# A decoder block on one core: 36 of the 44 up tiles of its two FFNs by seven half-size products instead of eight

## The chip, the cores and the metric

The kernel runs on one core of a Trainium2 chip. Its time is the device time of one execution in microseconds, the median of its runs. The profile is of one execution, with its own time. Engines are named as the profile names them: PE (matrix products) and PEld (its weight loads), DVE, ACT, POOL, and SP, which only issues DMAs here. A name with a q behind it is the engine's sequencer.

## The reference, cut to what matters

The block has a half-step SwiGLU FFN, a token-mixing layer (attention, a causal convolution, gates) and a second half-step SwiGLU FFN, over 512 tokens of width 1024. The FFN's hidden width is 2816. Each of the three is followed by a layer norm, and each is modulated by shift, scale and gate rows that come from a conditioning vector c by one product with `w_ada` (1024 x 9216).

```python
def swiglu(u, w_gu, w_down):
    a, g = jnp.split(u @ w_gu, 2, axis=-1)
    return (jax.nn.silu(a) * g) @ w_down

def reference(x, c, w_ada, b_ada, ffn1_w_gu, ...):
    mod = (jax.nn.silu(c) @ w_ada[l] + b_ada[l]).reshape(bsz, N_SUBLAYERS * N_MOD, 1, D_MODEL)
    sh1, sc1, g1, sh2, sc2, g2, sh3, sc3, g3 = [mod[:, i] for i in range(N_SUBLAYERS * N_MOD)]
    ...
    u = x * (1.0 + sc3) + sh3
    x = layer_norm(DEEPNORM_ALPHA * x + g3 * (MACARON_WEIGHT * swiglu(u, ffn2_w_gu[l], ffn2_w_down[l])), ...)
    return x
```

## The kernel before

**Precision.** Every float32 operand of a product is split into a high part, which PE's fast float format holds exactly, and the rest. A product of two matrices is then three matmuls per block of 128 channels: high by high, high by low, low by high (`dense`, L140 to L146). The tokens `u` are kept transposed, as `uh` and `ul`, eight blocks of 128 channels by 512 tokens.

**An FFN's up stage.** The hidden width is 22 tiles of 128. For a tile, two weight blocks of 128x1024 (512 KB each, one for a, one for g) are loaded by SP into the ring `raw` (3 buffers); ACT writes the high part `whi` (L113), POOL the low part `wlo` (L114), each in a ring of 5. PE makes 48 matmuls of 512 columns into two PSUM banks. Then ACT applies Silu (L396) and DVE multiplies by g from PSUM (L397); the result is the tile `sF`, kept in SBUF. The first FFN's first four tiles run together with the computation of u, while the weights arrive (`first_group`, L462 to L466). The second FFN's first two tiles are one group of products on 256 columns each, since u comes in four quarters of 128 tokens.

**Background work.** The rows of shift, scale and gate are made beside the up tiles by a queue of small tasks: `bg(n)` runs the next n of them in program order, `prefetch(n)` issues loads. A task is either one 128x1024 multiply-add on DVE (L222) or two 128x512 multiplications with a sum (L189), each on one 512 KB load of SP, held in a ring of three buffers (`ADA`). In the first FFN 32 such tasks make g1, g2, sh2 and sc2; in the second, 8 make g3 (ring of two). `load_x` brings in the four x tiles, which ACT scales (L491), and `finish_x(2)` multiplies and adds the layer norm's rows to them on POOL beside the second FFN's up tiles.

**An FFN's down stage** (`down`). For each of 22 hidden tiles, POOL multiplies the weight block by the gate row (L137), ACT writes its high part, DVE its low part, `part` splits `sF` into `sh` (ACT, L419) and `sl` (DVE, L420), and PE makes 24 matmuls (L355) into eight PSUM banks that stay open to the end. The rings of `sh` and `sl` hold five tiles each, and the casts of the first five `sF` run early in the up stage, as soon as those tiles exist.

**What sets the order.** The kernel is written in program order; a scheduler then orders each engine's instructions ahead of the run by its own estimates, subject to data, buffer and stated dependencies. Each engine runs its list in that order, so an instruction that waits holds up all behind it on its engine.

## Time and profile before

| | |
|---|---|
| median of 3 runs | 1339.79 us (1338.65 to 1344.78) |
| the profiled execution | 1338.98 us, span 1337.3 us, mean granted PE clock 0.992 |
| first FFN: start and u; up tiles 4 to 21; down | 0 to 66.7 us; to 264.5 us; to 374 us |
| mixing layer, with its output product | to 971.9 us |
| second FFN: up tiles; down and the last layer norm | to 1208.5 us; to 1337.3 us |
| moved by DMA | 197.88 MB |

The span is the time from the first instruction to the last; the execution's own time is 1.7 us longer. A timeline's row reads: start, duration, engine, line, operation, output <- inputs, shape; a bracket holds the idle time ahead of it and what released it. Matmuls overlap: what counts is the time from start to start. A row of a line's own view gives least, median and largest duration in ns. A row of windows gives for each stretch the busy time of PE, PEld, DVE, ACT and POOL with the number of instructions, then the granted clock, the DMA engines' busy share and GB/s.

### The profile page before, as it was taken

The numbers are of one execution on the slowest core, as the hardware profiler recorded it, in microseconds if no ns is written. First come the engines' busy times: TensorE is split into PE (matmuls) and PEld (weight loads), VectorE is DVE, ScalarE is ACT, GpSimd is POOL, SyncE is SP. The second block draws the span as 40 slices with busy tenths as digits, with TensorE's granted clock in tenths as the row PEclk, the third lists the DMA queues.
The fourth block names the chain that finished last, engine by engine and source line by source line (L and its number), as shares of the span: only waits on it lengthen the run. The fifth ranks groups of instructions, "written<-read, shape, count | busy, mean of one in ns | idle before, by whom it ended". The sixth has DMA issues, their size and how long they took to land.

```text
span 1337.3 us, 16794 instructions
## 1 busy us (share of the span) xinstructions
PE 1292.0 (97%) x6444; PEld 1069.7 (80%) x6444; DVE 737.6 (55%) x1017; ACT 523.0 (39%) x793; POOL 570.9 (43%) x392
## 2 busy tenths in 40 slices
PE   5899999999999999999999998998999999999997
PEld 4688888888898878778778876887898888888885
DVE  7886830354463959598788977025672000025545
ACT  2233322222266554655565547432452222222220
POOL 3465444744312565543442111142254566564434
PEclk9999999999999999999999998998999999999999
DMA  9668843223337574755567997972183233333321
GB/s 356 215 216 310 295 155 95 95 95 104 88 92 189 112 158 94 169 121 123 109 142 151 257 248 196 208 168 79 52 294 95 95 110 95 113 105 92 101 64 63
DMA packets 57856, 197.88 MB, mean 148 GB/s; under 512 B 6688, under 2 KB 6832, under 8 KB 57776
## 3 DMA queue, kind: packets, MB, share of 16 engines
q1 hardware_dynamic: 47952, 161.15, 36.3%
q0 software_dynamic: 9824, 35.66, 15.8%
q8 instruction: 50, 0.82, 0.2%
q14 instruction: 30, 0.25, 0.1%
HBM read 194.70 MB, written 2.10 MB: 147 GB/s over the span
## 4 chain that ended last, share of the span: by engine, by line
PE 82%; DVE 12%; DMA 3%; ACT 1%; POOL 1%; issue 1%; SPq 0%; DVEq 0%; POOLq 0%; ACTq 0%
PE y L355 19%; DVE cacc L525 4%; DVE ada L189 3%; DMA ada<-in_ada_t 1%; PE z L628 1%; PE q L144 1%; PE glub L144 1%; PE glua L144 1%; PE pw L650 1%; PE ycv L146 1%; PE gb L146 1%; PE gb L144 1%; PE ycv L144 1%; PE gb L145 1%; PE ycv L145 1%; PE q L145 1%
## 5 line engine op out<-in xcount | busy, mean ns | idle before, releaser
L114 POOL TENSOR_TENSOR wlo<-raw,whi 128x1024 fp32r<-128x1024 f32 x88 | 224.5, 2556 | 250.9 <-ACT whi L113 237.3
L113 ACT CAST whi<-raw 128x1024 fp32r<-128x1024 f32 x144 | 149.6, 1046 | 274.8 <-issue 50.6
L137 POOL TENSOR_TENSOR raw<-raw,mod_g 128x1024 f32<-128x1024 f32 x52 | 131.4, 2530 | 140.2 <-DMA raw<-in_dn 79.3
L525 DVE SCALAR_TENSOR_TENSOR cacc<-h,cv_w,cacc 128x512 f32<-128x512 f32 x232 | 173.8, 807 | 0.0
L114 DVE TENSOR_TENSOR wlo<-raw,whi 128x1024 fp32r<-128x1024 f32 x56 | 106.5, 1902 | 26.7 <-ACT whi L113 26.7
L130 ACT CAST whi<-raw 128x1024 fp32r<-128x1024 f32 x68 | 71.4, 1049 | 126.7 <-PE ga L145 19.7
L355 PE MATMUL y<-whi,sh 128*128 128x512 f32 x352 | 113.7, 390 | 0.0
L355 PE MATMUL y<-whi,sl 128*128 128x512 f32 x352 | 113.6, 389 | 0.0
L355 PE MATMUL y<-wlo,sh 128*128 128x512 f32 x352 | 113.6, 389 | 0.0
L189 DVE SCALAR_TENSOR_TENSOR ada<-ada,crow 128x512 f32<-128x512 f32 x96 | 91.7, 993 | 25.8 <-DMA ada<-in_ada_t 20.5
L640 POOL TENSOR_TENSOR be<-be,nb 128x127 f32<-128x127 f32 (+1 forms) x64 | 55.1, 861 | 102.0 <-DVE nb L635 100.5
L420 DVE TENSOR_TENSOR sl<-sF,sh 128x512 fp32r<-128x512 f32 x44 | 45.3, 1031 | 85.1 <-ACT sh L419 85.1
L419 ACT CAST sh<-sF 128x512 fp32r<-128x512 f32 x44 | 27.1, 623 | 144.4 <-PE y L355 132.0
L355 PEld LDWEIGHTS y<-whi,sl 128*128 128x128 f32 x352 | 66.1, 188 | 13.8
L355 PEld LDWEIGHTS y<-whi,sh 128*128 128x128 f32 x352 | 66.1, 188 | 13.6
L355 PEld LDWEIGHTS y<-wlo,sh 128*128 128x128 f32 x352 | 66.1, 188 | 13.6
L132 POOL DMA_DIRECT2D wlo<-in_w_in x44 | 38.4, 874 | 82.1 <-ACT wlo L131 78.3
L131 ACT ACTIVATE wlo<-whi 128x1024 fp32r<-128x1024 f32 x68 | 72.1, 1060 | 0.9
L635 DVE TENSOR_TENSOR_SCAN nb<-nb,future 128x127 f32<-128x127 f32 (+1 forms) x64 | 60.2, 941 | 2.0 <-ACT nb L633 1.8
L638 POOL TENSOR_SCALAR_AFFINE_SELECT be<-be 128x128 f32<-128x128 f32 x64 | 44.2, 691 | 22.9 <-ACT be L634 22.3
L222 DVE SCALAR_TENSOR_TENSOR acc<-ada,silu_c,acc 128x1024 f32<-128x1024 f32 x21 | 42.6, 2029 | 12.9 <-DMA ada<-in_ada_w 12.7
L654 DVE TENSOR_TENSOR wTl<-pw,wTh 128x128 fp32r<-128x128 f32 (+1 forms) x64 | 30.5, 477 | 32.5 <-ACT wTh L653 32.4
(496 smaller groups left out, 3366.8 us busy)
## 6 DMA issues: line engine op xcount, KB each, us to landing
raw<-in_gu SPq DMA_DIRECT2D x80, 512.0 KB, 3.6
raw<-in_w_in SPq DMA_DIRECT2D x48, 512.0 KB, 3.7
raw<-in_dn SPq DMA_DIRECT2D x44, 512.0 KB, 3.5
wlo<-in_w_in POOLq DMA_DIRECT2D x44, 512.0 KB, 7.1
ada<-in_ada_t SPq DMA_DIRECT2D x32, 512.0 KB, 5.3
ada<-in_ada_w SPq DMA_DIRECT2D x24, 512.0 KB, 4.9
ada<-in_ada SPq DMA_DIRECT2D x32, 256.0 KB, 6.0
raw<-in_gu_first SPq DMA_DIRECT2D x8, 512.0 KB, 6.5
```

Source lines behind the costliest of these rows:

```text
L113: nc.scalar.copy(hi, raw)
L114: lo_eng.tensor_sub(lo, raw, hi.bitcast(F32))
L130: nc.scalar.copy(hi, raw)
L131: nc.scalar.mul(lo, hi.bitcast(F32), -1.0)
L137: nc.gpsimd.tensor_mul(raw, raw, G)
L144: nc.tensor.matmul(ps[:, c0:c1], wh[:, ks], mov(uh, k)[:, c0:c1], start=(k == 0), stop=False)
L189: nc.vector.scalar_tensor_tensor(raw[:, qs], raw[:, qs], 1.0, crow[:, qs], ALU.mult, ALU.mult, accum_out=parts[:, q : q + 1])
L355: nc.tensor.matmul(acc[t][h][:, c0 - h * 512 : c1 - h * 512], st[:, tsl], wt[:, c0:c1], start=(k == 0 and i == 0 and c0 % 512 == 0), stop= ...
L420: nc.vector.tensor_sub(sl, sF[f], sh.bitcast(F32))
L525: ins = nc.vector.scalar_tensor_tensor(o, hv, cv_w[:, j, i : i + 1], o, ALU.mult, ALU.add)
L635: nc.vector.tensor_tensor_scan(nb[:, 1:n][:, ::-1], nb[:, 1:n][:, ::-1], future[:, S - n + 1 : S][:, ::-1], 1.0, ALU.mult, ALU.max)
L640: nc.gpsimd.tensor_mul(be[:, 0 : n - 1], be[:, 0 : n - 1], nb[:, 1:n])
```

## The change

The weights and tokens of an up tile's product are cut into 2x2 blocks: the weights into a and g (rows) by the first and last 512 input channels (columns), the tokens into those channels by the first and last 256 tokens. Eight block products make a tile; Strassen's algorithm, in Winograd's form, needs seven, on sums and differences of blocks. The two FFNs' tiles from the pair on (6 to 21 in the first, 2 to 21 in the second, 36 in all) go this way; the others are made as before.

- **Products** (`product`, L513). Seven groups of 12 matmuls with 256 columns: 84 instead of 48 with 512. Three PSUM banks per tile: q collects P1, P6, P7, P4 in turn without being cleared, v has P2, z collects P5 and P3. ACT copies q's partial sum out three times (`copied`, 128x256); DVE adds the parts (L540, L553, L562), ACT applies Silu to the whole tile, and DVE multiplies by g in two halves (L564 from PSUM, L565).
- **Weights** (`prep`, L486). Each tile needs seven weight halves of 128x512: A11, A12, A22 as loaded, and S1 to S4. ACT writes all seven high parts. The low parts of S1 and S3 are made on DVE, of S2 and S4 on POOL (`LO_POOL`, L503). For A11, A12 and A22, ACT writes the negated high part and POOL issues a DMA that adds the weights from memory to it (256 KB each, L501). POOL makes S1 and S2 in place (L505, L506), DVE S3 and S4 (L508, L509). A half is prepared nine products ahead; ten half slots in the rings; a fourth `raw` buffer; a tile's two loads are issued when S4 of the tile two before it is done.
- **Tokens** (`strassen_tokens`). The four sums of token blocks are made once for each FFN: 20 instructions of 128x512 on DVE, 8 on POOL, 8 casts on ACT (`replace`, which writes the last sum over u's second half, is among them). In the first FFN they stand ahead of the pair's products in the program and run beside these; in the second they come behind the pair.
- **Room.** In the first FFN the sums T1 and T2 lie where the x tiles lie later, so `load_x` moves into the down stage (k = 4, 6, 8, 10 in program order). `sh` and `sl` lie in a pool that opens when the up stage's own pool is closed. `finish_x(2)` moves to DVE in the second FFN's down stage, one task per k. The ring for g3's loads has one buffer instead of two.

In the lists below, as the scheduler left them, a row has the line, the operation, and output <- inputs with the tile's number behind each name. Where the program's line is the same in both versions, it stands a few lines later in the new one (L114 is L116, L189 is L192, L222 is L225).

POOL at the start of the first FFN's Strassen tiles, new: the last two low parts of the pair (`wlo_608`, `wlo_614`), token sums (`tsum`), S1 of the first two tiles (L505), and as the last row the first adding DMA.

```order
L430 TENSOR_TENSOR tsum_525<-ul_80 128x512
L432 TENSOR_TENSOR tsum_527<-uh_79 128x512
L116 TENSOR_TENSOR wlo_608<-raw_605,whi_607 128x1024
L434 TENSOR_TENSOR tsum_526<-ul_80 128x512
L437 TENSOR_TENSOR tsum_527<-tsum_527,tsum_526 128x512
L116 TENSOR_TENSOR wlo_614<-raw_611,whi_613 128x1024
L505 TENSOR_TENSOR raw4_743<-raw4_743 128x512
L430 TENSOR_TENSOR tsum_531<-ul_80 128x512
L432 TENSOR_TENSOR tsum_533<-uh_79 128x512
L505 TENSOR_TENSOR raw_741<-raw_741 128x512
L434 TENSOR_TENSOR tsum_532<-ul_80 128x512
L501 DMA wlo_735<-in_gu1 128x512
```

The same place before: from the second low part of tile 4 on, only low parts stand there.

```order
L114 TENSOR_TENSOR wlo_549<-raw_546,whi_548 128x1024
L114 TENSOR_TENSOR wlo_615<-raw_612,whi_614 128x1024
L114 TENSOR_TENSOR wlo_621<-raw_618,whi_620 128x1024
L114 TENSOR_TENSOR wlo_684<-raw_681,whi_683 128x1024
L114 TENSOR_TENSOR wlo_690<-raw_687,whi_689 128x1024
```

`wlo_735` is the low part of A11, the first product's weights; the DMA that completes it now stands behind seven token sums, two block sums and the pair's low parts.

DVE over one of the first FFN's Strassen tiles, new: sums of parts (L540, L553, L562), S3 and S4 (L509), low parts (L503), the products with g (L564, L565), and four background tasks (L225, L192).

```order
L540 TENSOR_TENSOR sF9_1118<-c1_1133,v_1116 128x256
L553 TENSOR_TENSOR u3_1109<-u3_1109,z_990 128x256
L509 TENSOR_TENSOR raw_740<-raw_741,raw_740 128x512
L225 SCALAR_TENSOR_TENSOR acc_1508<-ada_1768,silu_c_66,acc_1508 128x1024
L503 TENSOR_TENSOR wlo_735<-raw_740,whi_730 128x512
L225 SCALAR_TENSOR_TENSOR acc_1508<-ada_1895,silu_c_66,acc_1508 128x1024
L192 SCALAR_TENSOR_TENSOR ada_2021,parts_2160<-ada_2021,crow_84 128x512
L562 TENSOR_TENSOR sF8_991<-u2_1057,z_990 128x256
L192 SCALAR_TENSOR_TENSOR ada_2021,parts_2160<-ada_2021,crow_84 128x512
L564 TENSOR_TENSOR sF8_991<-sF8_991,q_988 128x256
L565 TENSOR_TENSOR sF8_991<-sF8_991,u3_1109 128x256
L503 TENSOR_TENSOR wlo_737<-raw_741,whi_732 128x512
```

Before, between the products with g of tiles 8 and 9 (a row with x2 stands for two alike):

```order
L397 TENSOR_TENSOR sF8_882<-sF8_882,h8g_833 128x512
L189 SCALAR_TENSOR_TENSOR ada_1475,parts_1469<-ada_1475,crow_84 128x512 x2
L189 SCALAR_TENSOR_TENSOR ada_1477,parts_1469<-ada_1477,crow_84 128x512 x2
L189 SCALAR_TENSOR_TENSOR ada_1548,parts_1469<-ada_1548,crow_84 128x512 x2
L189 SCALAR_TENSOR_TENSOR ada_1620,parts_1469<-ada_1620,crow_84 128x512
L397 TENSOR_TENSOR sF9_950<-sF9_950,h9g_901 128x512
```

In both, some four background tasks stand to a tile at this place, more than the one or two that the program's own order has; in the new list low parts and block sums that PE's next products need stand between and behind them.

ACT at the end of the first FFN's up stage, new: L563 is the last tile's Silu, L699 scales an x tile, L627 is the cast to `sh`.

```order
L699 ACTIVATE x3_3264<-x3_3264 128x1024
L115 CAST whi_3001<-raw_2998 128x1024
L563 ACTIVATE sF21_2685<-sF21_2685 128x512
L699 ACTIVATE x0_3033<-x0_3033 128x1024
L627 CAST sh_2857<-sF0_534 128x512
L627 CAST sh_2892<-sF1_537 128x512
```

The same place before; the casts of the first five `sF` stand some sixty rows earlier:

```order
L396 ACTIVATE sF20_1757<-h20a_1707 128x512
L113 CAST whi_1928<-raw_1925 128x1024
L113 CAST whi_1963<-raw_1960 128x1024
L396 ACTIVATE sF21_1831<-h21a_1781 128x512
L113 CAST whi_2002<-raw_1999 128x1024
L419 CAST sh_2041<-sF5_674 128x512
```

The first operand of the down stage, `sh_2857`, is now cast behind the last Silu and behind the scaling of x0.

The diff, cut to its core:

```diff
--- before.py
+++ after.py
...
+LOAD_X = (4, 6, 8, 10)
+LO_POOL = ("S2", "S4")
...
-    def finish_x(which):
+    def finish_x(which, pool=None):
...
-            row[v] = raw_tile(a[f"ln{which}_{v}"].broadcast_to([P, D]))
+            src = a[f"ln{which}_{v}"].broadcast_to([P, D])
+            if pool is None:
+                row[v] = raw_tile(src)
+            else:
+                row[v] = pool.tile([P, D], F32, tag="r", name="lnrow", bufs=2)
+                load(row[v], src)
...
+            eng = nc.gpsimd if pool is None else nc.vector
+            op = eng.tensor_mul if v == "g" else eng.tensor_add
...
-    def down(nk, part, w_src, G, tok_done):
+    def down(nk, part, w_src, G, tok_done, every=False):
...
-            if k % 2:
+            if k % 2 or every:
                 bg(1)
+            if nk == NF and not every and k in LOAD_X:
+                load_x(LOAD_X.index(k))
...
+    def make_temps(fp):
+        state["temps"] = [fp.tile([P, S], F32, tag="sF", name="tsum", bufs=NF) for _ in range(12)]
+    def strassen_tokens(up, u, homes):
+        uh, ul = u
...
+        v, g = nc.vector, nc.gpsimd
+        later = []
+        for c in range(2):
+            cs = slice(2 * c, 2 * c + 2)
+            f1, f2, f4, g1, g2, f3 = [t.rearrange("p (k s) -> p k s", k=2) for t in state["temps"][6 * c : 6 * c + 6]]
...
+            v.tensor_sub(f1, h["12"], h["11"])
+            g.tensor_sub(g1, l["12"], l["11"])
+            v.tensor_add(f1, f1, g1)
+            g.tensor_sub(f3, h["22"], h["12"])
+            v.tensor_sub(f2, h["22"], f1)
+            g.tensor_sub(g2, l["22"], l["12"])
+            v.tensor_add(f2, f2, l["22"])
+            v.tensor_sub(f4, h["21"], f2)
+            g.tensor_add(f3, f3, g2)
+            v.tensor_add(f4, f4, l["21"])
+            for x, f in (("2", f2), ("1", f1), ("4", f4)):
+                nc.scalar.copy(th[x], f)
+                v.tensor_sub(tl[x], f, th[x].bitcast(F32))
+            later.append((cs, f3, h["12"]))
+        def replace():
+            for cs, f3, h12 in later:
+                nc.scalar.copy(H["12"][:, cs], f3)
+                v.tensor_sub(L["12"][:, cs], f3, h12)
...
+        return replace, {"P1": part("11"), "P2": part("21"), "P3": part("22"), "P4": both("4"), "P5": both("1"),
+                "P6": both("2"), "P7": part("12")}
+    def strassen(up, fp, which, wgu, js, T, sF, between):
+        his = [wts.tile([P, 1024], F32R, align_bytes=256, tag="whi", name="whi", bufs=5) for _ in range(5)]
+        los = [wts.tile([P, 1024], F32R, align_bytes=256, tag="wlo", name="wlo", bufs=5) for _ in range(5)]
+        raws = [wts.tile([P, 1024], F32, tag="raw", name="raw", bufs=3) for _ in range(3)]
+        raws.append(up.tile([P, 1024], F32, name="raw4"))
...
+        order = []
+        for i in range(len(js) + 1):
+            order += [(x, k) for x, k in (("A11", i), ("A12", i), ("S1", i - 1), ("S2", i), ("A22", i - 1),
+                                          ("S4", i - 1), ("S3", i)) if 0 <= k < len(js)]
...
+            ra, rg = raws[2 * i % 4], raws[(2 * i + 1) % 4]
+            load(ra, a[wgu][js[i], 0])
+            load(rg, a[wgu][js[i], 1])
+            quarters[i] = {"A11": ra[:, :512], "A12": ra[:, 512:], "A21": rg[:, :512], "A22": rg[:, 512:]}
+        def prep(n):
...
+            x, i = order[n]
+            if n == 0:
+                fetch(0)
+                fetch(1)
+            q = quarters[i]
+            hi, lo = W[x, i] = slot(n)
+            r = q[{"S1": "A21", "S2": "A11", "S3": "A11", "S4": "A12"}.get(x, x)]
+            nc.scalar.copy(hi, r)
+            if x[0] == "A":
...
+                nc.scalar.mul(lo, hi.bitcast(F32), -1.0)
+                nc.gpsimd.dma_start(out=lo, in_=src, accum_op=ALU.add)
+            else:
+                (nc.gpsimd if x in LO_POOL else nc.vector).tensor_sub(lo, r, hi.bitcast(F32))
+            if x == "A12":
+                nc.gpsimd.tensor_add(q["A21"], q["A21"], q["A22"])
+                nc.gpsimd.tensor_sub(q["A11"], q["A21"], q["A11"])
+            elif x == "S2":
+                nc.vector.tensor_sub(q["A12"], q["A12"], q["A11"])
+                nc.vector.tensor_sub(q["A11"], q["A22"], q["A11"])
+            elif x == "S4":
+                fetch(i + 2)
+        def product(i, p, ps, x, first):
+            prep(st["n"] + 9)
+            st["n"] += 1
+            wh, wl = W.pop((x, i))
+            more = {} if first else {"skip_group_check": True}
+            for k in range(4):
+                ks = slice(k * P, (k + 1) * P)
+                th, tl = T[p](k)
+                nc.tensor.matmul(ps[:, :256], wh[:, ks], th, start=(first and k == 0), stop=False, **more)
+                nc.tensor.matmul(ps[:, :256], wh[:, ks], tl, start=False, stop=False, **more)
+                nc.tensor.matmul(ps[:, :256], wl[:, ks], th, start=False, stop=(k == 3), **more)
...
+        def P1(i):
+            st[i] = {x: bank(x) for x in "qvz"}
+            st[i]["s"] = fp.tile([P, S], F32, tag="sF", name=f"sF{js[i]}", bufs=NF)
+            product(i, "P1", st[i]["q"], "A11", True)
+            st[i]["c1"] = copied(st[i]["q"], "c1")
+        def P2(i):
+            d = st[i]
+            product(i, "P2", d["v"], "A12", True)
+            nc.vector.tensor_add(d["s"][:, :256], d["c1"], d["v"][:, :256])
+        def P6(i):
+            product(i, "P6", st[i]["q"], "S2", False)
+            st[i]["u2"] = copied(st[i]["q"], "u2")
...
+        def P5(i):
+            d = st[i]
+            product(i, "P5", d["z"], "S1", True)
+            nc.vector.tensor_add(d["u3"], d["u3"], d["z"][:, :256])
+        def P3(i):
+            d = st.pop(i)
+            product(i, "P3", d["z"], "S4", False)
+            s = d["s"]
+            nc.vector.tensor_add(s[:, 256:], d["u2"], d["z"][:, :256])
+            nc.scalar.activation(s, s, AF.Silu)
+            nc.vector.tensor_mul(s[:, :256], s[:, :256], d["q"][:, :256])
+            nc.vector.tensor_mul(s[:, 256:], s[:, 256:], d["u3"])
+            sF[js[i]] = s
+        st["n"] = 0
+        for n in range(9):
+            prep(n)
+        for i in range(len(js) + 1):
+            between(i, True)
+            for f, k in ((P1, i), (P2, i), (P5, i - 1), (P6, i), (P4, i - 1), (P3, i - 1), (P7, i)):
+                if 0 <= k < len(js):
+                    f(k)
+            between(i, False)
     def ffn(which, u, wgu, wdn, gate, first_done, tok_done):
...
-            while j < NF:
-                first = which == 2 and j < 2
-                n = 1 + j % 2 if which == 1 else 1
-                prefetch(n)
...
+            if which == 2:
+                make_temps(fp)
+                j = 0
+            up_cm, up = open_pool(f"up{which}")
+            def home(x, p):
+                if which == 1 and x in "12":
+                    return core.tile([P, 4, 256], F32R, tag=f"x{2 * '12'.index(x) + 'hl'.index(p)}", name=f"T{x}{p}")
+                return up.tile([P, 4, 256], F32R, name=f"T{x}{p}")
...
+            if which == 1:
+                replace, T = strassen_tokens(up, u, home)
+            prefetch(1)
+            pss = dense_group(names, srcs, u, which == 2)
...
+            if which == 2:
+                replace, T = strassen_tokens(up, u, home)
+            replace()
+            j += 2
+            def between(i, before):
+                n = 1 + (which == 1 and i % 3 != 0)
+                (prefetch if before else bg)(n if which == 1 or len(background) > 2 * NT else 0)
+            strassen(up, fp, which, wgu, list(range(j, NF)), T, sF, between)
+            close_pool(up_cm)
+            dn_cm, dp = open_pool(f"dn{which}")
+            state["dp"] = dp
 
...
-                sh = fp.tile([P, S], F32R, align_bytes=256, tag="sh", name="sh", bufs=RES + 1)
-                sl = fp.tile([P, S], F32R, align_bytes=256, tag="sl", name="sl", bufs=RES + 1)
+                sh = dp.tile([P, S], F32R, align_bytes=256, tag="sh", name="sh", bufs=RES + 1)
+                sl = dp.tile([P, S], F32R, align_bytes=256, tag="sl", name="sl", bufs=RES + 1)
...
-            down(NF, part, lambda f: a[wdn][f], mods[gate], tok_done)
+            down(NF, part, lambda f: a[wdn][f], mods[gate], tok_done, which == 2)
+            close_pool(dn_cm)
...
-        ada_row(lnp3, ada_ring(lnp3, 2), lnp3, "g3", 2, 0.5)
-        background.extend(finish_x(2))
+        ada_row(lnp3, ada_ring(lnp3, 1), lnp3, "g3", 2, 0.5)
+        background.extend(finish_x(2, lnp3))
...
-                last["rows"] = ln_rows(lnp3, 3)
+                last["rows"] = ln_rows(state["dp"], 3)
...
```

More of the change, by code (lines that the diff above doesn't have):

```diff
@@ L400, in ffn @@
             j = first_done(gated, fp)
-            while j < NF:
-                first = which == 2 and j < 2
-                n = 1 + j % 2 if which == 1 else 1
-                prefetch(n)
-                pairs = [j, j + 1] if first else [j]
-                names = [f"h{i}{x}" for i in pairs for x in "ag"]
-                srcs = [a[wgu][i, x] for i in pairs for x in range(2)]
-                pss = dense_group(names, srcs, u, first)
-                for q, i in enumerate(pairs):
-                    gated(i, pss[2 * q], pss[2 * q + 1])
-                j += len(pairs)
-                bg(n)
-                if which == 1 and j > NF - 2 * NT and j % 2:
-                    load_x(j // 2 - (NF // 2 - NT))
+            if which == 2:
+                make_temps(fp)
+                j = 0
@@ new lines, in ffn @@
+            up_cm, up = open_pool(f"up{which}")
[3 more added lines that the diff above has]
+                return up.tile([P, 4, 256], F32R, name=f"T{x}{p}")
+            pairs = [j, j + 1]
+            names = [f"h{i}{x}" for i in pairs for x in "ag"]
+            srcs = [a[wgu][i, x] for i in pairs for x in range(2)]
+            if which == 1:
+                replace, T = strassen_tokens(up, u, home)
```

42 lines of the change are left out of this document (40 added, 2 removed).

## The prediction

> **What bounds the kernel now.** The page's busy times and its chain come first.
>
> ```profile
> PE 1292.0 (97%) x6444; PEld 1069.7 (80%) x6444; DVE 737.6 (55%) x1017; ACT 523.0 (39%) x793; POOL 570.9 (43%) x392
> PE 82%; DVE 12%; DMA 3%; ACT 1%; POOL 1%; issue 1%; SPq 0%; DVEq 0%; POOLq 0%; ACTq 0%
> ```
>
> PE is busy for 97% of the span and holds 82% of the chain. The windows by stage say whether that holds where the change is: the two up stages, then two short stretches with dense DMA. Columns: length, PE, PEld, DVE, ACT, POOL, granted clock, DMA share, GB/s.
>
> ```profile
> 66.68:264.47 197.79, 197.79 (x873) 163.72 (x872) 103.78 (x123) 58.94 (x71) 106.98 (x41) 1.00 0.57 197
> 971.90:1208.40 236.50, 236.13 (x1111) 198.31 (x1110) 52.05 (x45) 68.90 (x87) 134.63 (x54) 1.00 0.39 127
> 100.00:134.00 34.00, 34.00 (x151) 28.15 (x150) 23.84 (x20) 10.85 (x13) 17.80 (x7) 1.00 0.86 311
> 735.00:770.00 35.00, 35.00 (x156) 29.00 (x155) 31.82 (x56) 20.93 (x23) 5.31 (x6) 1.00 0.98 252
> ```
>
> In both up stages PE never pauses and the clock is full, so fewer PE cycles are worth their full length there, as long as the others keep up. But the first FFN's early tiles already have DVE at 23.84 of 34 us and DMA at 0.86: that is where the slack is thin.
>
> **What the change removes.** Starts of matmuls, from PE's timeline: the first of tile 4 and of tile 5, 48 matmuls of 512 columns apart; and the first and last of 48 matmuls of 256 columns in the second FFN's pair.
>
> ```profile
> 66.68 0.39 PE L144 MATMUL h4a<-uh,whi 128*128 128x512 f32 x1
> 77.56 0.39 PE L144 MATMUL h5a<-uh,whi 128*128 128x512 f32 x1
> 88.44 0.39 PE L144 MATMUL h6a<-uh,whi 128*128 128x512 f32 x1
> ...
> 972.10 0.28 PE L145 MATMUL h1a<-ul,whi 128*128 128x256 f32 x1
> 977.74 0.28 PE L144 MATMUL h0a<-uh,whi 128*128 128x256 f32 x1
> 989.87 0.40 PE L144 MATMUL h2a<-uh,whi 128*128 128x512 f32 x1
> ```
>
> A tile takes 77.56 - 66.68 = 10.88 us, 0.2267 us a matmul. With 256 columns, (977.74 - 972.10) / 47 = 0.120 us, in the very pattern of weights (high, high, low) that the new products have. So a Strassen tile is 84 x 0.120 = 10.08 us, and 36 tiles save 36 x 0.80 = **28.8 us**: an eighth fewer products, of which the halved width gives part back (0.120 against 0.113).
>
> **What a tile now asks of the other engines.** Rows for each kind of instruction, and two from the DMA views (queue: packets, MB, share of 16 engines; the first over 66 to 170 us, the second over the run).
>
> ```profile
> L189 DVE SCALAR_TENSOR_TENSOR ada<-ada,crow x96: 635/682/2912, 6.8 to 833.3; 128x512 f32<-128x512 f32 x96
> L222 DVE SCALAR_TENSOR_TENSOR acc<-ada,silu_c,acc x21: 1273/1289/3417, 71.3 to 999.6; 128x1024 f32<-128x1024 f32 x21
> L420 DVE TENSOR_TENSOR sl<-sF,sh x44: 681/693/2901, 68.8 to 1301.4; 128x512 fp32r<-128x512 f32 x44
> L654 DVE TENSOR_TENSOR wTl<-pw,wTh x64: 258/474/693, 435.4 to 725.0; 128x128 fp32r<-128x128 f32 x16, 128x256 fp32r<-128x256 f32 x16, 128x384 fp32r<-128x384 f32 x16, 128x512 fp32r<-128x512 f32 x16
> L337 POOL TENSOR_TENSOR o<-o,lnb 128x512 f32<-128x512 f32 x2 | 2.6, 1281 | 0.2
> L132 POOL DMA_DIRECT2D wlo<-in_w_in x44: 856/875/892, 408.2 to 871.0; - x44
> DMA to landing us min/median/max: 5.4/6.9/9.7
> L419 ACT CAST sh<-sF x44: 619/622/642, 68.2 to 1300.7; 128x512 fp32r<-128x512 f32 x44
> q1 hardware_dynamic: 7826, 28.48, 77.8%
> q0 software_dynamic: 9824, 35.66, 15.8%
> ```
>
> ACT: seven casts, three negations and a Silu of 512 at 0.62 and three copies of 256 at about 0.4 (between 0.26 and 0.69 of L654's widths): 8.0 us of 10.08. POOL: four sums at 1.28 and three DMA issues at 0.88: 7.8 us. DVE: four of 512 at 0.69 and five of 256 at 0.4: 4.8 us. DMA: queue q1 was busy 77.8% of 104 us for 54.3 loads of 512 KB, 1.49 us each; q0, which adds to what lies there, 15.8% of 1337.3 us for 68 of 512 KB, 1.55 us per 256 KB. So a tile is 2 x 1.49 + 3 x 1.55 = 7.6 us. Each fits, though none by much. About 26 tiles carry nothing else; I cost them at **1 us** together (0 to 8: were one engine to need 10.4 us, 26 x 0.3). This hides under PE; ACT is the nearest to showing.
>
> The down stage of the second FFN gets the work of `finish_x(2)` on DVE, eight tasks of 1.3 us: L420's and the low part's 1.9 us leave over 2 us of a k's 5.4. No cost.
>
> **The first FFN's early tiles.** Here four background tasks stand in each tile, for some seven tiles. Each is one 1.29 or two 0.68: with the ends overlapping as the rows above allow, some 1.25 us. DVE is then at 4.8 + 4 x 1.25 = 9.8 us of 10.08. Two rows show what a collision with POOL costs (POOL's four L114, DVE's three L222, in the same stretch):
>
> ```profile
> 85.57 12.21 POOL L114 TENSOR_TENSOR wlo<-raw,whi 128x1024 fp32r<-128x1024 f32 x4 [3.36 <-ACT whi L113]
> 85.18 7.97 DVE L222 SCALAR_TENSOR_TENSOR acc<-ada,silu_c,acc 128x1024 f32<-128x1024 f32 x3
> ...
> L114 POOL TENSOR_TENSOR wlo<-raw,whi x88: 2388/2402/3398, 11.2 to 1188.3; 128x1024 fp32r<-128x1024 f32 x88
> L397 DVE TENSOR_TENSOR sF<-sF,h4g x2: 673/681/689, 83.2 to 1022.8; 128x512 f32<-128x512 f32 x2
> ```
>
> Undisturbed, DVE's three are 3.9 us and POOL's four 9.6; together they take 12.2, so each DVE instruction put (12.21 - 9.61) / 3 = 0.87 us into POOL's row, and waited up to (7.97 - 3.87) / 3 = 1.4 us itself, over half of a POOL instruction. L397, with one operand from PSUM, never stretched. POOL's four sums in a tile would hold DVE for about 4 x 1.28 x 0.57 = 2.9 us, at most 5.1, if each meets one; half of them do, by DVE's share: 1.5. So DVE needs 11.3 us, 1.2 over PE's. DMA needs 7.6 + 4 x 1.49 = 13.6 us, or, at the 413 GB/s of its best slices (below), 3.9 MB in 9.5 us: between 0 and 3.5 over. DVE's own list is what turns lateness into a PE wait: L553 must have read bank z before P3 may go on in it, and only two products, 2.9 us, stand between. The lead of nine halves doesn't help there; nor is it there yet after the start below. Whatever of the two is later holds a tile by 1.2 to 3.5 us, seven times, less 2.9: 5.5 to 21. I take **12 us**, about the middle; low end 0, where DMA keeps its best rate and the collisions stay few.
>
> ```profile
> DMA packets 7833, 28.57 MB, mean 275 GB/s; under 512 B 874, under 2 KB 874, under 8 KB 7826
> GB/s 181 285 202 0 126 413 361 296 14 202 153 303 225 343 321 356 366 328 258 326 359 399 296 72 399 214 405 413 386 175 350 243 321 293 307 262 142 224 326 343
> ```
>
> The mean over those 104 us (275) and the slices of 2.6 us (413 at best, over 350 for three in a row at most) say how far 3.9 MB in 10 us, 390 GB/s, lies from what was held for long.
>
> **Start of the first FFN's tiles.** The third matmul of P1 needs the DMA behind the token sums of POOL's list. Today POOL does the pair's second low part at:
>
> ```profile
> 68.37 2.41 POOL L114 TENSOR_TENSOR wlo<-raw,whi 128x1024 fp32r<-128x1024 f32 x1 [2.03 <-ACT whi L113]
> ```
>
> From there three low parts (7.2) and nine sums (9 x 1.28 = 11.5) lead to 87.1, and landing takes 5.4 at the least (512 KB; half of it may be quicker, say 4): 91 to 92.5, where PE is ready at 88.44 plus 0.24. That is 2.4 to 3.8 us with no collision. DVE's 18 token sums run meanwhile; if each of POOL's nine meets one and loses 0.87 / 1.29 x 0.69 = 0.47 us, it is 4.2 more; up to 0.69 each and on the low parts too, 8.3. The second DMA, 0.9 + 1.3 us behind the first, costs another 0.8 over P1's 1.44. And a PE idle this long loses its clock:
>
> ```profile
> 806.99 1.12 PE L797 MATMUL ptb<-ident,cn 128*128 128x128 f32 x4 [7.26 <-DVE cn L786]
> ...
> 809.61 0.63 PE L145 MATMUL ysb<-pl,whi 128*128 128x512 f32 x1
> 810.04 0.63 PE L146 MATMUL ysb<-ph,wlo 128*128 128x512 f32 x1
> ```
>
> After 7.26 us of idleness the 512-column matmuls start 0.43 us apart, not 0.23, for the rest of some 6 us: about 2.8 us lost. The Trainium skill (TensorE: Matmul & The Clock Gate, HAM oscillation) says that idle gaps over about 3.4 us bring the slow clock; this row agrees. I take 3.2 + 4.2 + 0.8 + 1.8 = **10 us** (2.5 to 16).
>
> **Start of the second FFN's tiles.** T1 and T2 come behind u, which is complete at 979.8, and DVE's list has the product with g of tile 1 ahead of sixteen instructions that end with T2's second half; that product waits for the pair's end.
>
> ```profile
> 979.09 0.69 DVE L293 TENSOR_TENSOR ul<-uf,uh 128x512 fp32r<-128x512 f32 x1
> ```
>
> From 989.9 that is 0.7 + 15 x 0.61 + 1.2 (a g3 task among them) to 1001.0. PE's list has 77 matmuls, 9.2 us, that can go first: 999.1. So 1.9 us without collisions; POOL does a dozen sums in that time, and sixteen waits of 0.47 give 7.5 more, of 0.87 13.9; with 1.6 to 2.8 for the clock, **11 us** (2 to 18). The Trainium skill (SBUF, two separate sides) calls the port pair of DVE and POOL an exclusive lock for whole instructions; with the full 1.28 of a POOL sum at every one of them it would be 22, and the sum 1360. The rows above show 1.4 of 2.4.
>
> **Ends of the up stages.** `sh` is now cast behind the last Silu. In the first FFN x0's load, which needs P5 of the last tile, and its scaling stand ahead too.
>
> ```profile
> L491 ACT ACTIVATE x<-x x4: 1060/1062/1063, 121.9 to 147.7; 128x1024 f32<-128x1024 f32 x4
> x<-in_x SPq DMA_DIRECT2D x4, 512.0 KB, 6.0
> raw<-in_dn SPq DMA_DIRECT2D x44, 512.0 KB, 3.5
> 264.47 0.61 PE L355 MATMUL y<-whi,sh 128*128 128x512 f32 x2
> ```
>
> Until now the down stage's first matmul follows at once (264.47). P5 ends two products, 2.9 us, ahead of the end; landing (6.0, or 3.5 as the down weights in that stage), scaling and cast come to 5.2 to 7.7, so PE waits 2.3 to 4.8: **3**. In the second FFN Silu and cast, 0.4 + 0.6 + 0.6: **2** (1 to 3).
>
> **Sum.** -28.8 + 10 + 12 + 3 + 11 + 2 + 1 = **+10.2 us**. The profiled execution took 1338.98 us (span 1337.3); its neighbour, the median of 1339.79, is 0.06% off. So 1338.98 + 10.2 = **1349 us**.
>
> **Rivals.**
> - *The others keep up* (faster). DMA holds its best rate, DVE's tasks fall between POOL's, and the starts stay near their low ends: starts 3 and 2, ends 3 and 2, the clock 3, the rest 1, in all 14 against 28.8, hence 1324. For it: PE waits nowhere in the up stages today, and 735 to 770 us has DMA at 0.98 and DVE at 31.82 of 35 with PE full. It decides if DVE needs under 10.1 us in the early tiles. Against it: four tasks a tile and 390 GB/s asked. Chance 0.28.
> - *Collisions serialize fully.* Every POOL sum holds DVE for its whole length, in both starts and in the early tiles: 16 + 18 + 7 x (9.8 + 5.1 - 10.08) - 3 = 65, with 3 + 2 + 1: 71 - 28.8, hence 1381. The rows show 0.57 of it at most where POOL is denser. Chance 0.12.
> - *256-column products cost more than half*, for instance by weight loads (PEld is 80% busy). At 0.13 us, 36 x 84 x 0.01 = 30 us, the whole saving: 1379. Against it: 48 in a row at 0.120. Chance 0.05.
>
> **How the numbers follow.** The forecast holds 0.55; its own bounds run from 1331 to 1367. The range takes in most of the faster case and some of the slow ones: 1320 to 1372. About 0.5% is what a measurement here tells from no change: 1333 to 1346.5. Of the forecast, 0.36 lies above, 0.17 within, 0.02 below; with the rivals (0.28 split 0.25 and 0.03; 0.17 above): faster 0.27, same 0.20, slower 0.53.
>
> **What would show it.** In the new profile: Strassen tiles 10.1 us apart late in either up stage (else the first term is wrong); PE idle at about 88 to 98 us, on the low part's DMA, and at 992 to 1010, on T2 or S2; tiles 12 us apart early in the first FFN, with PE waiting for DVE in bank z and DMA above 0.9; `y` waiting on `sh` at both ends. If PE stays full in the early tiles, the time is near 1335 or below, and the forecast fails there. If the starts wait under 5 us each, I have mis-sized the collisions.

## The result: 11% slower, and where the profile puts it

The changed kernel takes 1491.58 us (1485.96 to 1495.02, four runs) against 1339.22: a ratio of 1.1125 with a 95% interval of 1.1078 to 1.1172. The forecast was 1349, its range ended at 1372. The direction was right, the size was not: 152 us lost instead of 10.

The page of the changed kernel, busy times and chain:

```profile
PE 1318.7 (89%) x7740; PEld 1152.0 (77%) x7740; DVE 945.7 (63%) x1353; ACT 688.6 (46%) x1205; POOL 687.5 (46%) x580
PE 55%; DVE 11%; DMA 10%; POOL 8%; ACT 4%; issue 4%; POOLq 0%; DVEq 0%; SPq 0%; ACTq 0%
```

PE fell from 82% of the chain to 55%; DMA and POOL hold 18% of it, 4% before. No other engine is near full. The windows of its two up stages (columns as before):

```profile
66.88:335.98 269.10, 209.08 (x1450) 199.74 (x1448) 187.09 (x268) 131.14 (x252) 166.02 (x129) 0.89 0.71 196
1044.10:1356.60 312.50, 248.71 (x1830) 242.31 (x1828) 161.65 (x220) 158.69 (x311) 188.02 (x154) 0.90 0.58 141
```

They grew from 197.8 and 236.6 us to 269.1 and 312.5: 147 of the 152 us. The rest is 4.5 us in the second FFN's down stage and less than 1 us elsewhere. What PE waited for (us in total, times, longest):

```profile
PE q L522 <- ACT c L528: 72.1, 27, 11.0
PE z L522 <- DVE u L553: 20.5, 11, 5.2
PE q L522 <- ACT u L528: 12.0, 3, 6.1
PE q L524 <- DMA wlo<-in_gu: 9.2, 2, 6.2
```

With T1h and T1l (2.9 and 1.6 us) these are 118 us. The up stages lost 147 + 28.8 (the saving that didn't come) = 176, so some 58 us are left for the slow clock, which is granted at 0.89 and 0.90 there, 1.00 before. Counted from start to start, the matmuls of the two stages took 53 us more than at 0.2267 and 0.120 us each; the slow ones start 0.21 us apart. PE rarely waits for a weight; it waits for the copies of partial sums that free bank q. One of them, in ACT's and POOL's timelines around 248 us and, in PE's, the last matmul into bank q before the copy and the wait that the copy ends:

```profile
240.01 1.60 POOL L503 TENSOR_TENSOR wlo<-raw,whi 128x512 fp32r<-128x512 f32 x1
245.33 1.29 POOL L505 TENSOR_TENSOR raw<-raw 128x512 f32<-128x512 f32 x1 [3.72 <-DMA raw<-in_gu]
```
```profile
247.68 1.14 ACT L496 CAST whi<-raw 128x512 fp32r<-128x512 f32 x2 [3.02 <-DMA raw<-in_gu]
248.73 1.15 ACT L500 ACTIVATE wlo<-whi 128x512 fp32r<-128x512 f32 x2
249.78 0.35 ACT L528 COPY u<-q 128x256 f32<-128x256 f32 x1
250.55 0.37 ACT L528 COPY c<-q 128x256 f32<-128x256 f32 x1
```
```profile
246.13 0.28 PE L524 MATMUL q<-uh,wlo 128*128 128x256 f32 x1
250.98 0.39 PE L522 MATMUL q<-T2h,whi 128*128 128x256 f32 x1 [1.70 <-ACT c L528]
```

ACT's copy `c` could have run when that last product into q ended, at 246.4, but two casts of a later tile's weights stood ahead of it, and these waited for the load; two negations, the copy `u` and another cast stood there too. The longest pieces of the chain of waits from 241 to 256 us, one loop of it:

```profile
241.64 5.97 DMA raw<-in_gu
...
248.73 1.07 ACT wlo L500 x2
249.80 0.33 ACT u L528
250.13 0.52 ACT whi L496
250.65 0.27 ACT c L528
250.92 0.53 ACT whi L496
...
251.53 1.29 POOL wlo L503
...
252.93 0.89 POOL wlo L501
253.81 1.34 POOL wlo L503
...
255.17 5.23 DMA raw<-in_gu
```

From one load to the next are 13.5 us: landing (median 5.6 us in this kernel, 3.6 before), casts and negations on ACT, low parts and an adding DMA on POOL, and the last low part (of S4) frees the buffers for the next load. It runs once per tile, and PE needs 10.0 (the tiles of a1 and b1 below that wait for nothing). The busy times of ten late tiles say nothing of it:

```profile
1198.59:1329.60 131.01, 109.48 (x842) 106.97 (x841) 56.07 (x90) 70.55 (x144) 77.24 (x70) 0.95 0.60 138
```

DVE 5.6, ACT 7.1, POOL 7.7 us a tile of 13.1: each has room for more, and the tile is long all the same.

### The profile page after: what moved, and what is told of

Its sections match the earlier page's. It is cut to its first block, busy times and chain, and to the rows that moved or that the text cites. A ratio compares the mean times of both kernels' runs of the same rounds, so it can differ in the third digit from the quotient of the medians.

```text
span 1489.9 us, 20645 instructions
## 1 busy us (share of the span) xinstructions
PE 1318.7 (89%) x7740; PEld 1152.0 (77%) x7740; DVE 945.7 (63%) x1353; ACT 688.6 (46%) x1205; POOL 687.5 (46%) x580
## 4 chain that ended last, share of the span: by engine, by line
PE 55%; DVE 11%; DMA 10%; POOL 8%; ACT 4%; issue 4%; POOLq 0%; DVEq 0%; SPq 0%; ACTq 0%
PE y L364 17%; DMA raw<-in_gu 6%; DVE cacc L733 4%; POOL wlo L503 4%; POOL wlo L501 2%; PE q L522 2%; PE q L523 2%; ACT whi L496 2%; PE q L524 2%; DMA raw<-in_dn 1%; DMA ada<-in_ada_t 1%; PE z L836 1%; ACT wlo L500 1%; PE glub L146 1%; PE q L146 1%
## 5 line engine op out<-in xcount | busy, mean ns | idle before, releaser
L496 ACT CAST whi<-raw 128x512 fp32r<-128x512 f32 x252 | 148.7, 617 | 143.4 <-DMA raw<-in_gu 70.4
L139 POOL TENSOR_TENSOR raw<-raw,mod_g 128x1024 f32<-128x1024 f32 x52 | 133.1, 2563 | 141.0 <-DMA raw<-in_dn 91.8
L132 ACT CAST whi<-raw 128x1024 fp32r<-128x1024 f32 x68 | 71.4, 1050 | 126.5 <-PE ga L147 19.7
L503 POOL TENSOR_TENSOR wlo<-raw,whi 128x512 fp32r<-128x512 f32 x72 | 115.5, 1623 | 20.0 <-ACT whi L496 18.8
L116 DVE TENSOR_TENSOR wlo<-raw,whi 128x1024 fp32r<-128x1024 f32 x56 | 102.1, 1823 | 28.6 <-ACT whi L115 28.5
L522 PE MATMUL q<-T2h,whi 128*128 128x256 f32 x144 | 48.3, 335 | 72.1 <-ACT c L528 72.1
L501 POOL DMA_DIRECT2D wlo<-in_gu x108 | 98.0, 987 | 16.2 <-ACT wlo L500 11.4
L115 ACT CAST whi<-raw 128x1024 fp32r<-128x1024 f32 x72 | 74.7, 1044 | 60.9 <-POOL raw L139 20.6
L192 DVE SCALAR_TENSOR_TENSOR ada<-ada,crow 128x512 f32<-128x512 f32 x96 | 84.2, 907 | 24.8 <-DMA ada<-in_ada_t 19.1
L505 POOL TENSOR_TENSOR raw<-raw 128x512 f32<-128x512 f32 x36 | 50.1, 1391 | 104.0 <-DMA raw<-in_gu 79.1
L503 DVE TENSOR_TENSOR wlo<-raw,whi 128x512 fp32r<-128x512 f32 x72 | 77.7, 1082 | 25.1 <-ACT whi L496 21.9
L524 PE MATMUL q<-uh,wlo 128*128 128x256 f32 x288 | 84.3, 293 | 9.2 <-DMA wlo<-in_gu 9.2
L627 ACT CAST sh<-sF 128x512 fp32r<-128x512 f32 x44 | 26.5, 620 | 132.5 <-PE y L364 132.5
L522 PE MATMUL q<-uh,whi 128*128 128x256 f32 x288 | 84.4, 294 | 0.3 <-ACT u L528 0.3
L508 DVE TENSOR_TENSOR raw<-raw 128x512 f32<-128x512 f32 x36 | 27.9, 775 | 89.1 <-POOL raw L506 87.7
L523 PE MATMUL q<-ul,whi 128*128 128x256 f32 x288 | 84.0, 292 | 0.0
```

The lines of the kernel that those rows point to most:

```text
L115: nc.scalar.copy(hi, raw)
L116: lo_eng.tensor_sub(lo, raw, hi.bitcast(F32))
L139: nc.gpsimd.tensor_mul(raw, raw, G)
L192: nc.vector.scalar_tensor_tensor(raw[:, qs], raw[:, qs], 1.0, crow[:, qs], ALU.mult, ALU.mult, accum_out=parts[:, q : q + 1])
L496: nc.scalar.copy(hi, r)
L501: nc.gpsimd.dma_start(out=lo, in_=src, accum_op=ALU.add)
```

## The experiments

The stages are measured in PE's timeline: up 1 from the first matmul of tile 4, down 1 from the first into `y` to the mixing layer's first into `k`, up 2 from the first of tile 1, down 2 from the first into `y` to the end. A late tile is the mean of the second FFN's last ten distances between the first matmuls into bank v. All in us.

| run | time | up 1 | down 1 | up 2 | down 2, end | late tile |
|---|---|---|---|---|---|---|
| before | 1339 | 197.8 | 125.2 | 236.6 | 128.8 | |
| changed | 1492 | 269.1 | 125.4 | 312.5 | 133.3 | 13.1 |
| a1 no later loads | 1424 | 248.9 | 130.2 | 258.3 | 133.7 | 10.5 |
| a2 copies on DVE | 1496 | 279.1 | 126.8 | 307.6 | 132.4 | 13.2 |
| a3 no tasks in FFN 1 | 1471 | 253.4 | 126.6 | 306.3 | 133.7 | 13.2 |
| a4 loads in quarters | 1450 | 257.1 | 129.4 | 280.8 | 132.1 | 11.1 |
| b1 = a1 + a3 | 1382 | 212.9 | 127.7 | 259.4 | 132.7 | 10.1 |
| b2 quarters, A22 ahead | 1486 | 263.0 | 130.8 | 308.3 | 132.6 | 13.6 |
| b3 = b2 + tasks in order | 1478 | 257.8 | 134.4 | 304.5 | 132.2 | 13.4 |
| b4 = b3 + dense tiles | 1474 | 255.9 | 132.4 | 301.0 | 133.4 | 13.4 |
| c1 six raw | 1473 | 267.2 | 127.3 | 292.9 | 134.0 | 12.9 |
| c2 = c1 + tasks in order | 1476 | 261.1 | 133.1 | 294.8 | 134.8 | 12.5 |
| c3 = c2 + dense tiles | 1463 | 252.6 | 133.0 | 291.7 | 135.2 | 13.8 |
| d1 order held | 1578 | 305.2 | 132.9 | 356.7 | 134.1 | 15.6 |
| d2 = c1 + order held | 1466 | 264.1 | 130.0 | 289.0 | 132.2 | 11.8 |
| d3 = d2 + tasks in order | 1449 | 252.1 | 132.4 | 279.5 | 133.7 | 11.6 |
| e1 = d3, no POOL sums | 1402 | 230.0 | 134.1 | 253.0 | 135.7 | 10.1 |
| e2 = e1 + dense tiles | 1390 | 224.7 | 134.3 | 243.2 | 136.4 | 10.6 |
| e3 changed, no POOL sums | 1459 | 254.3 | 127.4 | 291.8 | 134.9 | 12.9 |
| f1 = b1, no token sums | 1357 | 194.3 | 128.6 | 249.6 | 132.9 | 10.1 |

Each is one execution beside one of the kernel before (1338 to 1339). The ideal, with the saving and no new wait, is 185.0 and 220.6 for the up stages and a span of 1308.5.

**The loop against its rivals.** a1 takes the load out of the loop:

```diff
-            load(ra, a[wgu][js[i], 0])
-            load(rg, a[wgu][js[i], 1])
+            if i < 2:
+                load(ra, a[wgu][js[i], 0])
+                load(rg, a[wgu][js[i], 1])
```

> Leaves out the loads of the gate and up weights from the third Strassen tile of each FFN on (the raw tiles are cast and summed again as they lie). Loop theory: a tile's rate is set by a loop of raw load, casts on ACT, sums and low parts on POOL, and the next load, 13.5 us against PE's 10.1; without the load (5 to 7 us of the loop) the Strassen tiles come every 10.1 to 11 us and the time falls to 1345 to 1390 us. Copy theory (the copies of partial sums stand behind casts on ACT, whatever these wait for): part of the waits stays, about 1430. Density theory (the prediction's: DVE and DMA too full beside the background tasks): only the first FFN's early tiles gain, about 1470.

a2 takes the copies off ACT (`nc.vector.tensor_copy` in `copied`), a3 replaces the four rows of the first FFN by `nc.vector.memset(v, 0.5)`:

> The three copies of partial sums per tile go from ACT to DVE. Loop theory: two copies leave the loop, 0.3 us each, so at best 20 us less, 1470 us; PE's wait is then on DVE's copies, or on casts, and tiles stay near 13 us. Copy theory: PE's waits on ACT's copies (84 us in all) go, about 1400 us. Density theory: DVE gets fuller, 1490 or more.

> Leaves out the 32 background tasks of the first FFN (rows g1, g2, sh2 and sc2 are set to a constant, their loads are gone). Loop theory: tiles in the second FFN, where hardly any task stands, already take 13.3 us, so the first FFN's come down from 14.3 to about 13 and the time to about 1470 us. Density theory: the first FFN's tiles fall to 10.1 us, 16 x 4 = 64 us less, about 1425 us.

b1 is a1 and a3 together:

> Leaves out both the later raw loads (as in the first run) and the first FFN's background tasks (as in the third). The first run left 64 us over the ideal 185 in the first FFN's up stage and 38 over 220.6 in the second. If density holds the early tiles once the loop is gone, the first FFN's up stage falls from 249 to about 205 us, with only its start left over, and the time to about 1380. If the early tiles are held by something else (the token sums' POOL and DVE work, adding DMAs), it falls by no more than the 16 us that leaving the tasks out gave before: about 1408.

a1 took 68 us away. Its time, 1424, is above the loop theory's 1345 to 1390 and near the copy theory's 1430; what speaks for the loop is that the second FFN's last nine tiles came every 10.0 us, and that PE's waits for ACT's copies fell from 84 to 32 us. Ten of its tiles, DVE, ACT and POOL as busy as before, with PE full:

```profile
1161.40:1266.20 104.80, 101.92 (x843) 101.50 (x842) 52.09 (x95) 75.25 (x143) 76.83 (x69) 0.98 0.53 86
```

The loads' traffic went with the loads in a1; e1 below has all of it, DMA at 0.81, and its late tiles take 10.0 us too, so it is not the traffic. a2 shows that the copies are where the wait appears and not what makes it: with them on DVE, PE waits 32 us for the copies, 47 for DVE's sum in bank z and 28 for casts, and nothing is won. a3 is worth 21 us in the changed kernel, but 42 where the loads are gone (b1, against its 44 expected): the two hide each other in the first FFN's early tiles. PE's wait for DVE's sum in bank z, the sign that the prediction named, in the first FFN's up stage of a1 and of b1:

```profile
PE z L523 <- DVE u L554: 23.9, 9, 5.2
PE z L523 <- DVE u L554: 0.5, 1, 0.5
```

So the density theory, which was the prediction's, names a real cost and not the main one. (The tasks' own loads go with them in a3 and b1; DVE's work and DMA's were not tried apart.)

**Room for the loads.** a4 loads quarters of a tile, each as soon as its own buffer is free; b2 also moves A22's cast ahead of S2's.

```diff
             elif x == "S4":
-                fetch(i + 2)
+                fetch(i + 3, "A12")
+            elif x == "A22":
+                fetch(i + len(rings["A22"]), "A22")
+            elif x == "S1":
+                fetch(i + 2, "A21")
+            elif x == "S3":
+                fetch(i + 2, "A11")
```

(That is b2. A22 has three buffers in its first FFN, two in its second and in a4; the copies of partial sums `c1` and `u3` have one buffer each where room was short.) Run c1 has six whole buffers instead, made of the fifth `whi` and `wlo`, and prepares seven halves ahead.

> Weights are loaded in quarters of a tile (256 KB), each as soon as its own buffer is free, and the second quarter of a has three buffers (two copies of partial sums have one buffer less to make room). The whole computation is there. Loop theory: each load is issued four to eight halves before it is used instead of two, the loop spans two tiles, and tiles come every 10.1 to 11.5 us: 1340 to 1400 us. Copy theory and density theory: within 20 us of 1490, with more DMA issues.

> Weights loaded in quarters as in the fourth run, with A22's cast placed ahead of S2's in the list of preparations, halves prepared eight products ahead instead of nine, and in the first FFN a third buffer for A22 too. Loop theory: in the fourth run a second loop was left (A22's load, A21+A22, S2, its cast, A22's cast, the next load; 11.2 us a tile), which now spans two tiles; the second FFN's late tiles come every 10.1 to 10.6 us, and the time is 1425 to 1440 (1450 in the fourth run). If it isn't this loop, the late tiles stay at 11.2 us.

> Six raw buffers instead of four, so a tile's two loads are issued three tiles ahead (behind S4 of the tile three before); room for them comes from the fifth buffer of each of whi and wlo, so halves are prepared seven products ahead instead of nine. The whole computation is there. Loop theory (each tile's load is issued two halves ahead of the first cast that needs it, and every engine's list has instructions that wait for it ahead of those that free PSUM): the load is now issued nine halves ahead, tiles without background tasks come every 10.0 to 10.6 us as without reloads, and the time is near the run without reloads, 1415 to 1435 us. If the lead of nine halves mattered and not the load, the time rises above 1490.

a4 won 42 us and a late tile of 11.1, as expected, but its time is above the 1340 to 1400. b2 and c1 missed. b2 lost a4's gain again: at 1238 us ACT's copy of u3 waits 5.3 us for a product on DVE, that one stands behind DVE's S4, which waits 5.6 us for POOL's S2, and POOL, ahead of S2, waits 5.0 us for a load. Which of its edits did it was not tried apart. In c1 two rows of POOL say why nine halves of room brought little:

```profile
1235.07 2.17 POOL L505 TENSOR_TENSOR wlo<-raw,whi 128x512 fp32r<-128x512 f32 x1
1244.09 1.29 POOL L507 TENSOR_TENSOR raw<-raw 128x512 f32<-128x512 f32 x1 [6.85 <-DMA raw<-in_gu]
```

The low part at 1235 frees a pair of buffers for the tile three on; the very next instruction in POOL's list is that tile's sum A21 + A22. The scheduler had moved it up by more than a tile, and POOL waited 6.85 us for a load that was issued a moment before. What PE itself waits for in c1 is DVE's sum in bank z, 65.8 us in all (20.5 in the changed kernel): POOL's held-up work then meets DVE's low parts, as the rows at the end of this text show.

**Order.** d1, d2 and d3 hold the preparations to the program's order, d1 with four buffers, d2 and d3 with six; the edit is one wrapper on each:

```diff
-            nc.scalar.copy(hi, r)
+            tc.keep_in_program_order(nc.scalar.copy(hi, r))
```

> The change as it is, but every instruction of the preparations (casts, negations, adding DMAs, low parts, block sums) is held to the program's order on its engine; four raw buffers, lead nine. In the changed kernel's list POOL's sum L505 of a tile stands directly behind the low part of S4 whose end lets that very tile be loaded. In the program's order the two adding DMAs of A11 and A12 stand between, and both need the same load. So, by the theory that needs room and order together: 1460 to 1490, little gained. If the order alone is at fault: 1425 or less.

> Six raw buffers (lead seven) and the preparations held to the program's order. Six buffers alone gave 1473 us: POOL's sum of the tile three on was put directly behind the low part that frees its buffers, so POOL waited up to 6.9 us for the load all the same. With the order held, nine halves lie between the load's issue and its first use: tiles without background tasks every 10.0 to 10.8 us, second FFN's up stage 258 to 270 us (293 with six buffers alone), time 1410 to 1435. If the lock of DVE by POOL is what stretches the tiles (a DVE low part took 4.7 us there), little changes: 1460 or more.

> As the run before, and the first FFN's background tasks held to the program's order too (one or two to a tile). If density holds the early tiles once loads don't: the first FFN's up stage loses 20 to 36 us against the run before, 1380 to 1410 us. Otherwise within 8 us of it.

Order alone made it worse than expected, 1578: the adding DMAs now stood behind the load too, and PE waited 95 us for them. Room and order together brought the regular late tile from 13 to 11.3 us, not to 10.0 as expected; d2's time, 1466, lies where its expectation put the lock of DVE by POOL (1460 or more). No engine waited for a raw load in the late tiles. What did hold them, in DVE's, POOL's and PE's timelines of d3:

```profile
1188.38 2.50 DVE L509 TENSOR_TENSOR wlo<-raw,whi 128x512 fp32r<-128x512 f32 x1 [1.27 <-ACT whi L501]
1190.80 0.41 DVE L559 TENSOR_TENSOR u<-u,z 128x256 f32<-128x256 f32 x1
```
```profile
1188.70 1.62 POOL L511 TENSOR_TENSOR wlo<-wlo 128x512 f32<-128x512 f32 x1
1190.40 1.62 POOL L512 TENSOR_TENSOR whi<-wlo,whi 128x512 f32<-128x512 f32 x1
```
```profile
1191.27 0.39 PE L528 MATMUL z<-uh,whi 128*128 128x256 f32 x1 [0.80 <-DVE u L559]
```

DVE's low part, 0.69 us elsewhere, lasted until POOL's sum was through; the sum that frees bank z stood behind it, and PE waited for that; the regular tile is 1.3 us longer than 10.0. That is the collision of the prediction, in tiles where it had not counted any.

**The port.** e1 takes POOL's sums away (`LO_POOL = ()`, and L505 and L506 on `nc.vector`) on top of d3, e3 in the changed kernel itself:

> As the last run (six buffers, preparations and tasks in the program's order), with all sums and low parts of the Strassen tiles on DVE; POOL is left with the adding DMAs there. In the last run a late tile took 11.3 us: DVE's low part of 0.69 us took 2.5 beside POOL's two block sums, and PE waited 1.3 us for the sum on DVE behind it. Lock theory: late tiles come every 10.0 to 10.3 us though DVE does 7.3 us a tile instead of 4.8; second FFN's up stage 250 to 260 us (279.6), time 1395 to 1425. If DVE's amount of work matters more than the lock: 11.3 us or more, time 1449 or above.

> The change as it is (four buffers, lead nine, the scheduler's order), with the Strassen tiles' sums and low parts on DVE instead of POOL. Loop theory: the loop from a load to the next keeps its load (5 to 7 us), but three POOL steps of 1.3 us in it become DVE steps of 0.6: late tiles 11 to 12.5 us instead of 13.4, time 1430 to 1470. If POOL's lock alone made the tiles long: 10.0 us and under 1400. If DVE was the fullest engine: above 1492.

e1 came out as expected. Ten late tiles of d3 and of e1:

```profile
1170.40:1286.30 115.90, 104.97 (x842) 100.88 (x841) 66.70 (x93) 71.79 (x144) 84.18 (x73) 1.00 0.71 152
```
```profile
1142.50:1243.40 100.90, 100.01 (x842) 99.81 (x841) 74.03 (x134) 72.81 (x144) 27.04 (x31) 1.00 0.81 179
```

DVE has more to do, 74 us in 101 instead of 67 in 116, and PE runs through. In d3's ten tiles nine of the twenty low parts on DVE took 2.5 us; in e1's, with four on DVE in each tile, all took 0.69 but one at the very end. POOL still issues adding DMAs there, and beside them DVE's rows keep their 0.69 us:

```profile
1159.96 0.87 POOL L506 DMA_DIRECT2D wlo<-in_gu  x1 [4.46 <-ACT wlo L505]
```
```profile
1160.21 0.69 DVE L509 TENSOR_TENSOR wlo<-raw,whi 128x512 fp32r<-128x512 f32 x1 [0.95 <-ACT whi L501]
```

A sum is also shorter on DVE (0.69 us) than on POOL (1.29), and that was not tried apart. The Trainium skill (SBUF — State Buffer, SBUF: two separate sides) has DVE and POOL share a port pair as an exclusive lock for whole instructions; d3's rows agree, DVE's instruction ends 0.56 us after POOL's (1188.70 + 1.62), about its own length. The section also says that whichever starts first has the pair; by these rows DVE's instruction started 0.32 us ahead of POOL's and still ended behind it. In e3 the loop kept its load, a late tile took 12.9 us (13.1 before, 11 to 12.5 expected), and the 32 us were won in other tiles: in the changed kernel the port is the smaller part.

**Starts and tasks.** b3 and c2 hold the first FFN's tasks to the program's order; b4, c3 and e2 put two more dense tiles ahead of each Strassen stage; f1 leaves out the token sums on top of b1 (`nc.scalar.copy(th[x], h["12"])` and the same for `tl` in their place).

> As the run with quarters and A22's cast ahead, and DVE's background tasks are held to the program's order (one or two to a tile of the first FFN, not four). Density theory for the early tiles: the first FFN's up stage loses another 15 to 35 us against that run. If density doesn't matter: within 5 us of it.

> As the run with six raw buffers, and DVE's background tasks held to the program's order (one or two a tile instead of four). Density theory for the first FFN's early tiles (36 us by the pair of runs without reloads): two tasks a tile leave DVE at 4.8 + 2.1 to 2.5 us of 10, so most of it goes: 1385 to 1405 us. If it's the tasks' presence and not their density: within 8 us of the run before.

> As the last run, with two more tiles of each FFN made by dense products ahead of the Strassen tiles (32 instead of 36 by Strassen), as cover for token sums and first weight halves. Costs 4 x 0.8 = 3.2 us of the saving. If the starts wait for sums and preparations that take their time whatever PE does, each start gains up to 20 us: 20 to 40 us less than the run before. If the start's waits come from the preparations' own loop, which begins only behind the dense tiles, nothing is gained: 0 to 5 us more.

> As the run before, with two more tiles of each FFN made by dense products ahead of the Strassen tiles, as cover for token sums and first halves. The starts hold some 28 and 38 us by the runs without reloads. If they wait for work that can run beside PE, 20 to 40 us less than the run before, 1345 to 1380; if the preparations begin only behind the dense tiles, 0 to 5 us more.

> As the run before, with two more dense tiles ahead of the Strassen tiles in each FFN. If the starts' waits are for token sums and first halves that can be made beside dense products: 10 to 30 us less than the run before. If not, 0 to 10 us more.

> As the run without later loads and without the first FFN's background tasks (1382 us), and the token sums are left out too (T1, T2 and T4 are plain copies of one block of u on ACT, and u's last block stays as it is). That run had 28 us over the ideal in the first FFN's up stage and 39 in the second's. If the token sums on DVE and POOL hold the starts: up stages of 187 to 197 and 225 to 240 us, 1330 to 1355 us. If the first weight halves hold them (low parts, adding DMAs, POOL's share of the pair): less than 10 us from each, 1365 or more.

The tasks' order was worth 12 us in the first FFN where loads did not hold the tiles (d3 against d2), 5 to 6 where they did (b3, c2), less than the 15 to 36 expected. Two dense tiles as cover were worth 3 to 13 us, where 20 to 40 (b4, c3) and 10 to 30 (e2) were expected. f1 took 19 us from the first FFN and 10 from the second: the first start is mostly the token sums, the second mostly is not. What holds the second (29 us over the ideal in f1) stays open in part; the first four tiles there are 11 to 17 us apart, in the stretch where g3's tasks with their one-buffer ring run too. PE's longest wait there, 4.35 us at 1026.8, is for DVE's sum in bank z, and DVE's list has two low parts of g3's own row ahead of it, which took 4.80 us beside POOL's sums. No run leaves g3's tasks out.

No version here beats the kernel before. The best that computes all of it, e2, is 52 us behind it, and 80 over the ideal of 36 tiles.

## Why the prediction was wrong, step by step

- **The saving** (28.8 us): right. A Strassen tile that waits for nothing takes 10.0 us (a1, b1, e1); 10.08 was worked out. It didn't show in the time, since the tiles had to wait.
- **"About 26 tiles carry nothing else; I cost them at 1 us together"**: the step that failed. The sums behind it were about right (ACT 8.0, POOL 7.8, DVE 4.8 predicted, 7.1, 7.7 and 5.6 measured), but busy times leave out a chain in which each step waits for the one before. The late tiles took 13.1 us; 26 such tiles lose some 26 x 3.0 = 78 us. There is a loop through the four raw buffers, one turn per tile: landing 5 to 6 us and 8 us of work on ACT and POOL. What shows it: a1 (10.0 us a tile without the load), and the chain above. The lead of nine halves is between preparation and product; the load is issued only two halves ahead of its first cast.
- **The wait that I named was not the largest.** I looked for lateness in DVE's sum for bank z: 20.5 us, 14.6 of them in the first FFN. For ACT's copies for bank q, which I had costed as busy time only, PE waited 84, of which 32 are left without the loads (a1): casts that wait for a load stood ahead of them.
- **Early tiles** (12 us): the named wait is there (23.9 us in a1, 0.5 without the tasks), its size was wrong. The tasks cost 42 us once the loads are gone, 21 beside them. Collisions with POOL, which I had counted in early tiles alone, also hold late ones (15 us of 116 in ten of them, d3 against e1).
- **Start of the first FFN** (10 us): the first wait, 6.2 us on the adding DMA, is close to the 7.4 worked out for it; then a second of 11.0, on ACT's copy behind a dozen casts, some of which waited for DVE's sums, was not seen. f1 gives the token sums 19 us.
- **Start of the second FFN** (11 us): too small. PE waited 15.4 us there in the changed kernel, 7.9 of them on ACT's copy, and 29 us over the ideal are left in that stage even in f1.
- **Ends** (3 and 2 us): PE waited 5.2 us in all for `sh` and 2.2 for `sl`, as forecast.
- **The clock**: forecast as 2 us at each start. It cost 53 to 58. It is granted at 0.89 and 0.90 over the two stages, where PE's waits reach 11.0 us, at 0.95 in the ten late tiles, where they reach 3.8, and at 1.00 in d3's, where they stay under 2.

Summed over spans: loads 67.6 us (a1), tasks 42.1 on top (b1), token sums 24.5 on top (f1), and 47 left: 29 in the second up stage, 9 in the first, 8 in the down stages, 1 in the mixing layer. This is one order of taking them out; in another the shares differ, as a3 shows.

## What to carry to other kernels

Busy time per tile against the bound engine's time is only half of the check: follow one buffer from its load to the instruction that frees it and back, on every engine's list, and divide by the number of tiles in flight. Where an engine both prepares later weights and drains PSUM, a preparation that waits for a load stops the drain, however far ahead it is meant to be; here room for the load together with a held order brought the regular tile from 13 to 11.3 us, while either alone left it at 12.9 or made it worse. And an engine with idle time can still cost the bound one through a shared port: moving POOL's sums onto DVE, which was busy for 67 of 116 us and then for 74 of 101, won 47 us.
